# First mixer of a hybrid decoder: two block inversions by joined inverses on VectorE, channel sums by matrix products, sample taps as products and row sums

## The chip, the cores and the metric

The kernel runs on one core of a Trainium2 chip. The metric is device time in microseconds of one launch, the median of several runs. Engines are named as in the profile: PE (TensorE), DVE (VectorE), ACT (ScalarE), POOL (GpSimd) and SP (SyncE, which issues transfers); PEld is PE's weight load.

## The reference

One inference step of a two-layer trunk for two groups that share weights: a prompt of 512 new tokens and 8 samples of 4 new tokens each, 544 tokens in all, 1024 channels, all in float32. Layer 0 mixes with a convolution beside a delta rule, layer 1 with a diagonal state-space system; a feed-forward follows each. What matters here is layer 0's mixer:

```python
p = x @ w_in
pa, pb = p[..., :2 * D_A], p[..., 2 * D_A:]
u = pa[..., :D_A] * sigmoid(pa[..., D_A:])
ext = concatenate([conv_state, u], axis=1)
ya = silu(layer_norm(causal_depthwise(ext, conv_w, conv_b), ln_g, ln_b))  # 31 taps, 512 channels
...
def step(s, inp):                        # delta rule, 8 heads of 64
    sa = einsum('bhvk,bhk->bhv', s, -kk_t)
    s = s * d_t + sa[..., None] * (kk_t * a_t)[:, :, None, :] + v_t[..., None] * k_t[:, :, None, :]
    return s, einsum('bhvk,bhk->bhv', s, r_t)
...
out = concatenate([ya, yb], axis=-1) @ w_out     # ya: convolution, yb: delta rule
```

## The kernel before

Channels stand on partitions, tokens along the rows: 512 prompt columns and 32 sample columns, in two halves of 256 and 288. Every weight product is made of three products of split operands (`xh`, `xl` with `whi`, `wlo`); the weights come as one stream through the whole kernel, and ACT and DVE split each chunk (`split`, L262 and L170).

The first mixer has four pairs of heads and four convolution tiles. For pair p, `pair_in` projects and shifts keys, rates and values, `pair_front` makes products within chunks of 64 tokens (`wkv_front`) and inverts unit lower triangular blocks of 16 (`wkv_solve`), `pair_mid` joins the blocks into inverses of 64 (`wkv_mid`, which reads `mn` from L801 on) and prepares the scan (`wkv_tail`), and `pair_out` runs the scan over 8 chunks, a group norm of the heads and the gate. `sample_front` and `sample_out` do the same for the samples, all heads at once. `conv_in` and `conv_taps` make tile i of the convolution, `conv_end` its layer norm over four tiles, the activation and the first half of the output projection (the k tiles of `ya`). `mixer_ab_out` adds the second half (the k tiles of `yb`).

`wkv_solve` moves blocks so that each stands on one partition: out to memory (`dx`), back into `xb`, 15 steps of a product (`stmp`) and a sum (`mm`) on POOL, a transposed copy (L782), out to memory (`dm`, L783) and back into `mn` (L787). All its transfers are on SP's queue. `xb` and `mm` have one buffer each.

`conv_taps` does 30 multiply-adds (L167) for the prompt columns and 30 for the sample columns, in turns, into `cacc`. `conv_end` sums the four tiles on POOL (into rows of `xres`, which is free until the residual is loaded), one product with a matrix of ones spreads the sum over the channels (L598), and the same again for the squares (L610).

The order of work comes from `weave`: generators are advanced in turns, each step has a priority of its turn plus a delay, and a scheduler orders the instructions of every engine from these priorities; at run time each engine takes its instructions in that fixed order. The delays and the weaves that matter:

```python
hi, md, lo = -4, -6, 8
weave((hi, pair_out(1)), (hi, pair_mid(2)), (md, pair_front(3)), (0, conv_in(3)), (lo, conv_taps(2)))
weave((hi, pair_out(2)), (hi, pair_mid(3)), (md, sample_front()), (lo, conv_taps(3)))
weave((hi, pair_out(3)), (hi, sample_out()), (0, conv_end()))
```

## Time and profile before

| | us |
|---|---|
| median of three runs | 1544.8 |
| lowest and highest run | 1542.68, 1547.15 |
| span of the profiled execution | 1542.7 |

The profile is one execution on the core; its span, from the first to the last instruction, equals the lowest run to the digits shown, so nothing has to be added around it. Times in the rows are microseconds from the span's start. Busy time of an engine doesn't count its register, branch, semaphore and transfer-issuing instructions. In a name such as `cacc<-usam,cols,cacc` the tile written stands left of the arrow. Products with float32 operands leave two records each. `[3.75 <-DMA mn<-dm]` behind a row says that the engine stood idle that long before it, and what ended the wait. The first mixer runs from the start to about 381 us, its layer norm to about 447 us.

### The profile page before, as it was taken

What the parts mean: (1) busy time and instruction counts of PE and PEld (TensorE: products, weight loads), DVE (VectorE), ACT (ScalarE), POOL (GpSimd) and SP (SyncE); (2) the same over time, 40 slices, a digit from 0 to 9 for tenths busy, and PEclk for the clock granted to TensorE, in tenths of its full rate; (3) what the DMA queues carried; (4) which work ended last, traced back from release to release, by engine and by line L of the source; (5) the groups of instructions that cost most, each with busy time, mean ns of one, the idle gap of its engine ahead of it and who ended that gap; (6) DMA issues with size and microseconds to landing.
All of it is one profiled execution on the core that took longest, in us unless ns stands there. A gap on an engine that the chain in (4) does not pass through costs nothing.

```text
span 1542.7 us, 31307 instructions
## 1 busy us (share of the span) xinstructions
PE 1445.0 (94%) x12064; PEld 1374.1 (89%) x12064; DVE 1013.4 (66%) x2513; ACT 616.9 (40%) x1407; POOL 353.9 (23%) x492
## 2 busy tenths in 40 slices
PE   7999999789799999999999789999899999999996
PEld 6988887577789999999899778899899999999996
DVE  6688796766879955557884856754675555554335
ACT  5444352251264444443232435553454444442222
POOL 1252552611540200002561622102420000000102
PEclk9999999689899999999999789999999999999997
DMA  5222113111213232225563367832222222232321
GB/s 192 73 65 67 39 54 100 22 38 58 99 37 118 89 127 89 84 85 164 165 182 116 111 178 210 219 107 96 67 69 89 90 89 85 88 92 86 84 68 58
DMA packets 128340, 152.43 MB, mean 99 GB/s; under 512 B 46512, under 2 KB 71856, under 8 KB 127936
## 3 DMA queue, kind: packets, MB, share of 16 engines
q1 hardware_dynamic: 105232, 120.11, 25.7%
q10 hardware_dynamic: 20800, 22.46, 4.6%
q0 software_dynamic: 2160, 7.87, 1.6%
q8 instruction: 95, 1.56, 0.4%
q14 instruction: 53, 0.43, 0.1%
HBM read 128.17 MB, written 22.22 MB: 97 GB/s over the span
## 4 chain that ended last, share of the span: by engine, by line
PE 71%; DVE 11%; DMA 6%; POOL 4%; issue 3%; ACT 3%; SPq 1%; ACTq 0%; DVEq 0%; POOLq 0%
PE ps_mm L192 61%; PE ps_wk L192 3%; POOL stmp L170 2%; DVE xres L170 2%; POOL mm L170 2%; DVE wlo L170 2%; DVE xres L167 1%; DMA tm<-dk 1%; DVE s5a L170 1%; PE ps_wf L725 1%; ACT xres L164 1%; DVE ln_t L167 1%; PE ps_wk L1089 1%; DMA dg<-s5a 1%; DMA ye<-dy 1%
## 5 line engine op out<-in xcount | busy, mean ns | idle before, releaser
L192 PE MATMUL ps_mm<-xh,whi 128*128 128x256 f32 (+1 forms) x2016 | 492.1, 298 | 21.9 <-ACT whi L262 6.5
L192 PE MATMUL ps_mm<-xl,whi 128*128 128x256 f32 (+1 forms) x2016 | 493.2, 296 | 5.2 <-DVE xl L167 3.6
L192 PE MATMUL ps_mm<-xh,wlo 128*128 128x256 f32 (+1 forms) x2016 | 490.0, 295 | 0.0
L170 DVE TENSOR_TENSOR wlo<-wraw,whi 128x512 fp32r<-128x512 f32 x350 | 258.4, 740 | 272.3 <-ACT whi L262 270.1
L262 ACT CAST whi<-wraw 128x512 fp32r<-128x512 f32 x380 | 230.9, 611 | 514.7 <-PE ps_mm L192 448.9
L192 PEld LDWEIGHTS ps_mm<-xh,whi 128*128 128x128 f32 x2016 | 353.6, 195 | 29.4 <-ACT whi L262 6.8
L192 PEld LDWEIGHTS ps_mm<-xl,whi 128*128 128x128 f32 x2016 | 356.9, 195 | 14.3 <-issue 5.9
L192 PEld LDWEIGHTS ps_mm<-xh,wlo 128*128 128x128 f32 x2016 | 354.3, 194 | 4.6 <-issue 3.9
L192 PE MATMUL ps_mm<-fl,whi 128*128 128x256 f32 (+1 forms) x704 | 154.3, 290 | 0.0
L192 PE MATMUL ps_mm<-fh,whi 128*128 128x256 f32 (+1 forms) x704 | 153.7, 289 | 0.0
L192 PE MATMUL ps_mm<-fh,wlo 128*128 128x256 f32 (+1 forms) x704 | 153.6, 289 | 0.0
L192 PEld LDWEIGHTS ps_mm<-fh,wlo 128*128 128x128 f32 x704 | 115.7, 188 | 0.7 <-issue 0.6
L192 PEld LDWEIGHTS ps_mm<-fl,whi 128*128 128x128 f32 x704 | 115.8, 188 | 0.4 <-issue 0.4
L192 PEld LDWEIGHTS ps_mm<-fh,whi 128*128 128x128 f32 x704 | 115.5, 188 | 0.7 <-issue 0.6
L167 DVE SCALAR_TENSOR_TENSOR c<-ps_mm,cols,c 128x254 f32<-128x254 f32 (+3 forms) x264 | 98.1, 393 | 0.3
L167 DVE SCALAR_TENSOR_TENSOR cacc<-uext,cols,cacc 128x512 f32<-128x512 f32 x120 | 94.8, 790 | 2.5 <-ACT cacc L164 1.5
L170 POOL TENSOR_TENSOR ln_s<-xres 128x256 f32<-128x256 f32 (+1 forms) x8 | 10.3, 1301 | 313.8 <-DVE xres L170 313.8
L170 DVE TENSOR_TENSOR s5a<-s5a 128x64 f32<-128x64 f32 (+3 forms) x135 | 74.5, 574 | 9.0 <-DMA dg<-s5a 4.4
L170 DVE TENSOR_TENSOR c<-ps_mm,c 128x256 f32<-128x256 f32 (+1 forms) x88 | 35.3, 435 | 60.3 <-PE ps_mm L192 54.6
L170 POOL TENSOR_TENSOR s5a<-s5a 128x1024 f32<-128x1024 f32 (+2 forms) x19 | 48.1, 2532 | 49.9 <-DVE s5a L170 44.2
L170 POOL TENSOR_TENSOR wlo<-wraw,whi 128x512 fp32r<-128x512 f32 x30 | 41.5, 1390 | 77.7 <-ACT whi L262 74.2
L192 PE MATMUL ps_mm<-yh,whi 128*128 128x256 f32 (+1 forms) x240 | 57.4, 293 | 0.3 <-ACT sg L164 0.3
(368 smaller groups left out, 2064.2 us busy)
## 6 DMA issues: line engine op xcount, KB each, us to landing
wraw<-in_w_up SPq DMA_DIRECT2D x176, 256.0 KB
wraw<-in_w_down SPq DMA_DIRECT2D x80, 256.0 KB
wraw<-in_w_in_ab SPq DMA_DIRECT2D x44, 256.0 KB
wraw<-in_w_out_c SPq DMA_DIRECT2D x21, 256.0 KB
wraw<-in_w_out_ab SPq DMA_DIRECT2D x16, 256.0 KB
dg<-s5a ACTq DMA_DIRECT2D x8, 512.0 KB
df<-s5a ACTq DMA_DIRECT2D x8, 512.0 KB
gx<-dg POOLq DMA_DIRECT2D x8, 512.0 KB, 5.1
```

What stands on the lines that cost most here:

```text
L164: return self.nc.scalar.activation(out, in_, f, **k)
L167: return self.nc.vector.scalar_tensor_tensor(out, a, s, b, op0, op1)
L170: return (eng or self.nc.vector).tensor_tensor(out, a, b, op=op)
L192: ins = self.nc.tensor.matmul(*a, **k)
L262: self.nc.scalar.copy(hi, src)
L725: nc.tensor.matmul(pa[:, i], lhsT=flat(kb[HS[hd], c // 2, c % 2]), rhs=ar[HS[hd], :, c], start=True, stop=True)
L1089: gate = nc.tensor.matmul(pq[:, 4 * i + j:4 * i + j + 1], lhsT=t[:, b - P:b], rhs=self.con("ones")[:, 0:1], start=t is ts[0], stop=t is ts ...
```

## The change

Three parts of the first mixer are written anew; the rest of the kernel stays as it was.

1. The inversions of pair 3 and of the samples (`late`) go by joining: the inverse of a block of 2s comes from its two diagonal inverses of size s, for s = 2, 4, 8, with the 2-blocks written directly. Each level is a product per block, a row sum, a product per block, a row sum, all on DVE; the transposed copy is on ACT. The loads and returns of these two alternate between SP's and ACT's queues. Their products use a tile `spr` of one buffer.
2. The sample taps of a convolution tile become two POOL products over all 31 taps (two tokens of every sample at a time, into `spr`), two DVE row sums and a bias on ACT.
3. `conv_end` sums four tiles, and then their squares, by four products that accumulate in one bank; the POOL sums are gone, and it uses rows 3 to 7 of `xres` instead of 5 to 7.

`sample_front` moves from the weave of `pair_mid(3)` into that of `pair_front(3)`, at the same delay.

```diff
             self.act(ca, uext[:, 0:NP], AF.Identity, scale=w(0), bias=cb)
-            self.act(cs, usam[:, 0:32], AF.Identity, scale=w(0), bias=cb)
+            at = usam[:, 0:8]
+            o = COL["caw"] + i * 31
+            ws = self.cols[:, o:o + 31].unsqueeze(1).unsqueeze(1).broadcast_to([P, 2, NS, 31])
+            for j in range(0, NJ, 2):
+                pr = gp.tile([P, 512], F32, name="spr", tag="spr", bufs=1)
+                pr = pr[:, 0:2 * NS * 31].rearrange("p (j s t) -> p j s t", s=NS, t=31)
+                win = bass.AP(at.tensor, at.offset + NS * j, [at.ap[0], (NS, 2), (1, NS), (NS, 31)])
+                self.tt(pr, win, ws, ALU.mult, nc.gpsimd)
+                nc.vector.tensor_reduce(cs[:, NS * j:NS * j + 2 * NS].rearrange("p (j s) -> p j s", s=NS), pr,
+                                        mybir.AxisListType.X, ALU.add)
+            self.act(cs, cs, AF.Identity, bias=cb)
             for t in range(1, 31):
...
                 self.stt(ca, uext[:, t:t + NP], w(t), ca, ALU.mult, ALU.add)
-                self.stt(cs, usam[:, 8 * t:8 * t + 32], w(t), cs, ALU.mult, ALU.add)
             yield
...
             yield from self.wkv_front(d, dx)
-            yield from self.wkv_solve(dx, dm, 8, self.mn)
+            yield from self.wkv_solve(dx, dm, 8, self.mn, p == 3)
...
             yield from self.sample_in(g, dx)
-            yield from self.wkv_solve(dx, dm, 4, self.mns)
+            yield from self.wkv_solve(dx, dm, 4, self.mns, True)
...
         def conv_end():
-            s1, q, t = row(5), row(6), row(7)
+            s1, sqs = row(3), [row(4 + i) for i in range(4)]
             for h in range(2):
                 n, H = HB[h], HT[h]
-                self.tt(s1[:, H], cacc[:, 0, H], cacc[:, 1, H], ALU.add, nc.gpsimd)
-                for i in (2, 3):
-                    self.tt(s1[:, H], s1[:, H], cacc[:, i, H], ALU.add, nc.gpsimd)
                 pm = self.bank([P, 512], "wf")
-                nc.tensor.matmul(pm[:, :n], lhsT=self.con("ones"), rhs=s1[:, H], start=True, stop=True)
+                for i in range(4):
+                    nc.tensor.matmul(pm[:, :n], lhsT=self.con("ones"), rhs=cacc[:, i, H], start=i == 0, stop=i == 3)
                 for i in range(4):
                     self.stt(cacc[:, i, H], pm[:, :n], -1.0 / 512, cacc[:, i, H], ALU.mult, ALU.add)
-                    if i == 0:
-                        self.act(q[:, H], cacc[:, i, H], AF.Square)
-                    else:
-                        self.act(t[:, H], cacc[:, i, H], AF.Square)
-                        self.tt(q[:, H], q[:, H], t[:, H], ALU.add, nc.gpsimd)
+                    self.act(sqs[i][:, H], cacc[:, i, H], AF.Square)
                 yield
...
                 pv = self.bank([P, 512], "wf")
-                nc.tensor.matmul(pv[:, :n], lhsT=self.con("ones"), rhs=q[:, H], start=True, stop=True)
+                for i in range(4):
+                    nc.tensor.matmul(pv[:, :n], lhsT=self.con("ones"), rhs=sqs[i][:, H], start=i == 0, stop=i == 3)
                 root = self.act(s1[:, H], pv[:, :n], AF.Sqrt, scale=1.0 / 512, bias=self.eps(LN_EPS))
...
         weave((hi, pair_out(0)), (hi, pair_mid(1)), (md, pair_front(2)), (0, conv_in(2)), (0, after(4, pair_in(3))), (lo, conv_taps(1)))
-        weave((hi, pair_out(1)), (hi, pair_mid(2)), (md, pair_front(3)), (0, conv_in(3)), (lo, conv_taps(2)))
+        weave((hi, pair_out(1)), (hi, pair_mid(2)), (md, pair_front(3)), (md, sample_front()), (0, conv_in(3)), (lo, conv_taps(2)))
         nc.scalar.dma_start(out=O["shift"], in_=shout)
-        weave((hi, pair_out(2)), (hi, pair_mid(3)), (md, sample_front()), (lo, conv_taps(3)))
+        weave((hi, pair_out(2)), (hi, pair_mid(3)), (lo, conv_taps(3)))
         weave((hi, pair_out(3)), (hi, sample_out()), (0, conv_end()))
...
-    def wkv_solve(self, dx, dm, nu, mn):
+    def wkv_solve(self, dx, dm, nu, mn, late=False):
         nc, gp = self.nc, self.gp
...
         tmp = gp.tile([64, 64], F32, name="stmp", tag="stmp", bufs=2)
+        queue = lambda q: nc.scalar if late and q % 2 else nc.sync
         src = dx.rearrange("(q r) u c -> q u r c", r=16)
...
             b = q % nb
-            nc.sync.dma_start(out=xb[q * nu:(q + 1) * nu], in_=src[q][:, :, 16 * b:16 * b + 16])
+            queue(q).dma_start(out=xb[q * nu:(q + 1) * nu], in_=src[q][:, :, 16 * b:16 * b + 16])
         M = mm[:n, 0]
...
         nc.gpsimd.memset(mm[:n, 0].rearrange("p a b -> p (a b)")[:, 0:256:17], 1.0)
-        for j in range(15):
+        if late:
+            V = nc.vector
+            ap = lambda t, o, *d: bass.AP(t.tensor, t.offset + o, [t.ap[0], *d])
+            X = xb[:n]
+            V.tensor_copy(ap(M, 16, (34, 8)), ap(X, 1, (34, 8)))
+            for s in (2, 4, 8):
+                k, d = 8 // s, 34 * s
+                pr = gp.tile([P, 512], F32, name="spr", tag="spr", bufs=1)[:n, :k * s ** 3]
+                T = tmp[:n, :k * s * s]
+                for g in range(k):
+                    o, r = d * g, slice(g * s ** 3, (g + 1) * s ** 3)
+                    self.tt(pr[:, r].rearrange("p (i b j) -> p i b j", b=s, j=s),
+                            ap(X, o + s, (1, s), (0, s), (16, s)), ap(M, o, (0, s), (1, s), (16, s)), ALU.mult)
+                V.tensor_reduce(T, pr.rearrange("p (i j) -> p i j", j=s), mybir.AxisListType.X, ALU.add)
+                for g in range(k):
+                    o, r = d * g, slice(g * s ** 3, (g + 1) * s ** 3)
+                    self.tt(pr[:, r].rearrange("p (i b j) -> p i b j", b=s, j=s),
+                            ap(M, o + 17 * s, (16, s), (0, s), (1, s)), ap(T, g * s * s, (0, s), (1, s), (s, s)), ALU.mult)
+                V.tensor_reduce(ap(M, 16 * s, (d, k), (16, s), (1, s)),
+                                pr.rearrange("p (g i b j) -> p g i b j", g=k, i=s, j=s), mybir.AxisListType.X, ALU.add)
+            yield
+        for j in range(0 if late else 15):
             rows, cols = 15 - j, j + 1
...
                 yield
-        nc.gpsimd.tensor_copy(mm[:n, 1].rearrange("p a b -> p b a"), M)
+        if late:
+            nc.scalar.copy(mm[:n, 1].rearrange("p a b -> p b a"), M)
+        else:
+            nc.gpsimd.tensor_copy(mm[:n, 1].rearrange("p a b -> p b a"), M)
         nc.sync.dma_start(out=dm.rearrange("q u w r c -> (q u) (w r c)"), in_=mm[:n].rearrange("p w a b -> p (w a b)"))
...
             o = 64 * (q // nb) + 16 * b
-            nc.sync.dma_start(out=mn[o:o + 16, :, :, 16 * b:16 * b + 16].rearrange("r u w c -> r (u w) c"),
+            queue(q).dma_start(out=mn[o:o + 16, :, :, 16 * b:16 * b + 16].rearrange("r u w c -> r (u w) c"),
                               in_=dm[q].rearrange("u w r c -> r (u w) c"))
...
...
```

## Rows read from the trace of the kernel before

**Rows 1.** The page: the span, then busy time of each engine

```profile
span 1542.7 us, 31307 instructions
...
PE 1445.0 (94%) x12064; PEld 1374.1 (89%) x12064; DVE 1013.4 (66%) x2513; ACT 616.9 (40%) x1407; POOL 353.9 (23%) x492
```

**Rows 2.** By stretch: PE, PEld, DVE, ACT, POOL busy (instructions), clock, DMA, GB/s

```profile
251.00:297.00 46.00, 38.37 (x447) 28.17 (x446) 40.84 (x93) 12.71 (x29) 21.82 (x40) 0.83 0.22 60
297.00:320.00 23.00, 16.44 (x225) 11.81 (x225) 14.48 (x26) 10.72 (x23) 15.06 (x39) 0.72 0.15 32
320.00:381.00 61.00, 59.02 (x687) 48.81 (x686) 39.26 (x115) 14.97 (x40) 6.04 (x7) 0.95 0.14 46
```

**Rows 3.** Timeline of POOL, 200 to 385 us: start, duration, line, operation, [idle before it]

```profile
265.99 1.06 POOL L170 TENSOR_TENSOR xres<-xres,cacc 128x256 f32<-128x256 f32 x1
...
275.79 0.21 POOL L170 TENSOR_TENSOR stmp<-xb,mm 64x15 f32<-64x15 f32 x1 [2.69 <-DMA xb<-dx]
...
292.69 0.61 POOL L782 COPY mm<-mm 64x256 f32<-64x256 f32 x1
...
301.17 0.20 POOL L170 TENSOR_TENSOR stmp<-xb,mm 16x15 f32<-16x15 f32 x1 [2.76 <-DMA xb<-dxs]
...
316.79 0.60 POOL L782 COPY mm<-mm 16x256 f32<-16x256 f32 x1
```

**Rows 4.** Timeline of the SP queue, 200 to 330 us

```profile
270.89 2.88 SPq L770 DMA_DIRECT2D xb<-dx  x8
...
295.64 3.74 SPq L787 DMA_DIRECT2D mn<-dm  x8
```

**Rows 5.** Timeline of PE, 290 to 336 us

```profile
298.84 0.66 PE L801 MATMUL ps_wo<-mn,xa 64*64 64x64 f32 x4 [3.75 <-DMA mn<-dm]
...
302.48 1.60 PE L801 MATMUL ps_wo<-mn,xa 64*64 64x64 f32 x24
...
309.69 0.67 PE L610 MATMUL ps_wf<-xres,cons 128*128 128x256 f32 x2 [0.26 <-DVE cacc L167]
...
314.00 0.75 PE L610 MATMUL ps_wf<-xres,cons 128*128 128x288 f32 x2 [2.10 <-POOL xres L170]
...
319.63 0.58 PE L192 MATMUL ps_mm<-xh,whi 128*128 128x256 f32 x1 [1.97 <-ACT xh L262]
```

**Rows 6.** Timeline of DVE, 225 to 325 us

```profile
242.69 0.69 DVE L170 TENSOR_TENSOR z<-ps_wo,cons 128x512 f32<-128x512 f32 x1 [4.34 <-PE ps_wo L801]
...
265.36 3.03 DVE L167 SCALAR_TENSOR_TENSOR cacc<-uext,cols,cacc 128x512 f32<-128x512 f32 x3
...
296.11 0.75 DVE L167 SCALAR_TENSOR_TENSOR cacc<-uext,cols,cacc 128x512 f32<-128x512 f32 x1
...
312.78 1.75 DVE L612 RECIPROCAL xres<-xres 128x256 f32<-128x256 f32 x1 [1.21 <-ACT xres L164]
```

**Rows 7.** Timeline of DVE, 324 to 400 us

```profile
374.31 0.15 DVE L170 TENSOR_TENSOR rq_t<-rq_y 128x2 f32<-128x2 f32 x1
374.50 0.16 DVE L167 SCALAR_TENSOR_TENSOR rq_t<-rq_t,rq_x 128x2 f32<-128x2 f32 x1
```

**Rows 8.** Instructions that write cacc: duration in ns min/median/max, first and last start

```profile
L167 DVE SCALAR_TENSOR_TENSOR cacc<-usam,cols,cacc x120: 226/243/1348, 16.3 to 262.2; 128x32 f32<-128x32 f32 x120
```

**Rows 9.** POOL groups by shape, 0 to 390 us: busy, mean ns, idle before

```profile
L170 POOL TENSOR_TENSOR sm<-swv,cons 128x512 f32<-128x512 f32 x2 | 2.1, 1042 | 31.3 <-DVE swv L170 31.3
```

**Rows 10.** The chain that ended last: start, duration, what

```profile
19.02 1.46 DVE cacc L167 x9
```

**Rows 11.** The same chain, 200 to 450 us

```profile
320.21 3.74 PE ps_wo L840 x32
...
328.81 1.08 PE ps_wo L865 x32
...
330.77 1.02 PE ps_wo L859 x16
...
380.93 7.93 PE ps_mm L192 x40
```

## The prediction

> **What bounds the kernel now.** I read the page first: PE is busy for 94% of the span [rows 1], so a change pays only where PE stands still, runs at a lower clock, or has work taken away. Then the table by stretch for the end of the first mixer, where both late inversions stand. From 251 to 320 us PE is idle for 7.6 + 6.6 us and the granted clock is 0.83 and 0.72; from 320 to 381 us it is idle for 2.0 us at 0.95 [rows 2]. What could come back at most: 16.2 us of idle time, plus 38.4 x 0.17 + 16.4 x 0.28 + 59.0 x 0.05 = 14 us if all products there ran at the full one of the two levels (2.4 instead of 1.2 GHz). That is 30 us; no part of this change can be worth more in this stage.
>
> Then the timelines of this stretch, to see which waits end last. Two chains run side by side. The first is pair 3's inversion: its blocks lie in `xb` at 275.8, POOL needs until 293.3 for 31 small instructions (17.5 us) [rows 3], the result goes out and comes back in eight transfers that take SP 3.74 us to issue [rows 4], and PE, waiting 3.75 us, starts on it at 298.8 and gets the rest at 302.5 [rows 5]. The sample's inversion stands behind it, 301.2 to 317.4 on the same engine [rows 3]. The second is the convolution: the last prompt tap ends on DVE at 296.9 [rows 6], the layer norm over four tiles follows, with POOL sums between the sample's inversion steps (PE waits 2.1 us for one), and the first product of the output projection starts at 319.6, after 2 us of waiting for its operand [rows 5]. From there PE has 61 us of nearly gapless work up to 380.9, where the second half of the output projection begins [rows 11]. So the stage ends sooner if the point 319.6 comes sooner, or if work that now lies behind it is done in the idle time ahead of it.
>
> **The late inversions move to DVE.** Out: 31 POOL instructions for pair 3 and 31 for the sample. In, for each: one copy, then three levels of products and row sums, (4+1+4+1) + (2+1+2+1) + (1+1+1+1) = 20, together 21 DVE instructions, and the transpose as one ACT copy. Seventeen have at most 128 elements a row; dependent ones of that kind start 0.19 us apart [rows 7]: 3.2 us. Four read or write 512; a 128x512 product took 0.69 us [rows 6]: 2.8 us. So 6.0 us instead of 17.5 and 16.2. No `tensor_reduce` stands in the trace. Its bounds: as cheap as a small instruction (0.19), or as dear as the dearest one-input DVE row, the reciprocal, 1.75 us for 256 elements, 3.5 for 512 [rows 6]; an inversion then costs between 5 and 12 us. I take the product's price, because both stream 512 values through one instruction.
>
> The order changes too. The sample's front is woven beside pair 3's, and its solve is emitted first. `xb`, `mm` and `spr` have one buffer each, so pair 3's load waits until the sample's blocks were read, and its memset until the sample's inverse went out. I reckon pair 3's start as 3.5 us later for that (half of a solve, between nothing and one whole solve plus the 2.3 us from copy to first return transfer [rows 3, 4]). The two queues share the eight loads and the eight returns, which saves half of 2.88 and of 3.74 us of issue [rows 4], 3.3 us. With 17.5 - 6.0 = 11.5 us less in the solve and 3 us lost to taps that stand between its steps (four of 0.75 [rows 6]), the inverse reaches PE 11.5 + 3.3 - 3.5 - 3 = 8 us earlier, near 294. What queues behind: ACT's queue now holds waits for transfers (eight issues per solve), and the weight casts behind them; ACT is busy 12.7 of 46 us there [rows 2], so I price that at nothing, and at up to 2 us if casts stall PE.
>
> **Sample taps.** Out: 120 DVE instructions of 0.24 us [rows 8] and four ACT starts. In: eight POOL products of 496 elements, eight DVE sums, four ACT biases. Most of the 120 run far ahead of their turn (from 16.3 us on) in DVE's idle time and cost little; after 251 us only four are left. One place is on the chain: nine of them, 1.46 us at 19.0 [rows 10]; the new product reads the last window column, so it can't run there. Gain 1.5 us (between 0 and 2). A POOL product of this size took 1.04 us [rows 9]; the far bounds are the solve's smallest step, 0.20, and twice the price for its strided pattern. What hides them is POOL's free time: it is busy 21.8 of the 46 us before 297 even with pair 3's solve on it [rows 2]. Without that cover the solves of pairs 1 and 2, which stay on POOL, lose 2 us each.
>
> The Trainium skill (SBUF, State Buffer, section on the single rule of contention) says that a two-input VectorE operation and a GpSimd operation that reads SBUF lock each other out for a whole instruction. Here three taps took 3.03 us instead of 2.25 while two POOL sums ran [rows 3, 6], 0.4 us for each. By the rule the two POOL products of tile 3 would hold up its taps by 2.1 us, by the row by 0.8, and the gain would be 1.3 us smaller by the rule; I keep the row.
>
> **What DVE carries.** It was busy 40.8 of 46 us up to 297 [rows 2]. Added before the last tap: two solves 12.0, two sums 1.4, POOL's interference 0.8; gone: four sample taps, 1.0. Of the 5.2 idle us I let 4.2 fill. The last tap then ends at 296.9 + 9 = 306.
>
> **Layer norm.** Out: six POOL sums ahead of the first product pair and six ahead of the second. In: twelve more products with float32 operands; one costs PE 0.75 us at the clock of then [rows 5], 9 us in all, at most 18 at the lower level and about half when they follow each other. Three of four in the first group need only tiles 0 to 2 and run in idle PE time; that idle time is the cover, and without it the 9 us stand on PE. After the last tap: one product 0.75, four subtractions and squares that follow one another (two of a tap's length, 1.5), the last square's product 0.67, together 3 us, then as now from the end of the first half's product, 310.4, to 319.6: 9.3 us [rows 5]. So the projection starts at 306 + 12.3 = 318.3 instead of 319.6: 1.3 us gained. The row places 3 to 7 are held longer, and five loads of the residual wait on SP until the norm is through; tile 3 needs its row only three projection tiles later, so I price that at nothing, at 2 us if not.
>
> **Work pulled ahead.** With the inverse 8 us earlier and the sample's some 20 us earlier, PE does in front of 318 what stood behind it: the 32 products of 3.74 us, two times 16 and 32 products of about 1.0 and 1.1 us [rows 11], 7.9 us, and the sample's first products, which I put at 2 us (estimate: two groups of 16 like the sixteen of 1.02). Together 9.9 us of the 61. Bounds: 0, if that time is used up by waits, and 20, if the whole scan comes forward.
>
> **Sum.** 1.5 (start) + 1.3 (projection) + 9.9 (pulled ahead) = 12.7 us. The profiled span of 1542.7 equals the fastest of the three runs (1542.68), so nothing is added around it; the median of the runs, 1544.8, lies 2.1 above. 1542.7 - 12.7 + 2.1 = 1532.1.
>
> **Rivals.** (A) Both chains come forward fully: the solves slip between taps that had idle time anyway, the last tap ends at 300 and the clock stays up. The 12.7 us grow by 6 and by half of the 14 us of clock: 1519. For it: PE's low clock is in just this stretch. Against it: DVE has 5.2 idle us for 13 us of work. (B) Nothing measurable: pair 3 waits for the whole solve of the sample through the shared tiles. If the sample's blocks come as late as today's place behind pair 3's, the inverse of pair 3 lands near 301 again, the products pulled ahead shrink to the sample's 2 us, and 1.5 + 1.3 + 2 is left less 3 for ACT's waits: 1543. (C) Slower: DVE becomes the bound. If a solve costs 12 us (the dear row sums), the last tap ends at 318 instead of 306, the projection starts at 330, 10.7 us later than now, and 5 us are pulled ahead: 10.7 - 5 - 1.5 = 4 us slower, and 3 us more if POOL products delay the middle solves: 1549 to 1552. It decides from a last tap at about 312 on.
>
> **Chances.** Forecast 0.45, own range 1524 to 1538; A 0.12; B 0.23; C 0.20. A difference under 0.3% (4.6 us) can't be told from none: the three runs lie that far apart. Of B, 0.03 falls on the faster and 0.02 on the slower side. Faster 0.60, same 0.18, slower 0.22. The range goes from just under A, 1517, to C's upper end, 1552, which leaves out about 0.15.
>
> **What the new profile would show.** Right: DVE does `spr` products and sums for two solves in about 6 us each, POOL's `stmp` groups fall from 75 to 45, the inverse reaches PE (the products on `mn`) before 296, the last tap of tile 3 ends at 303 to 308, the first output projection product starts by 319, and the second half of the projection before 371 instead of 380.9. The step most likely to be wrong is the last tap's time: every DVE microsecond added ahead of it delays the projection. The forecast fails if that tap ends after 312, if a row sum of 496 elements costs well over 1 us, or if the pulled-ahead products still stand behind the projection's start in PE's order.

## The result, and the profile after

The changed kernel takes 1553.65 us (median of nine runs, 1547.29 to 1573.25), the kernel before 1545.81 us beside it (nine runs, 1541.54 to 1548.85). The ratio is 1.0057, with a 95% interval of 1.0034 to 1.0081: slower, where 1532.1 was forecast, and 1.65 us outside the range. In the ratios here and below, runs over 1.5% above the fastest of the same kernel are left out.

The page of the changed kernel and the three stretches answer to [rows 1, 2]:

```profile
span 1550.5 us, 31231 instructions
...
PE 1453.7 (94%) x12088; PEld 1381.7 (89%) x12088; DVE 1005.7 (65%) x2443; ACT 619.6 (40%) x1409; POOL 330.4 (21%) x426
```

```profile
251.00:297.00 46.00, 38.16 (x378) 27.02 (x377) 37.80 (x105) 11.82 (x27) 2.01 (x4) 0.75 0.12 28
297.00:320.00 23.00, 16.60 (x202) 11.96 (x202) 20.15 (x37) 9.69 (x20) 3.00 (x2) 0.83 0.25 62
320.00:381.00 61.00, 60.67 (x688) 51.55 (x689) 30.68 (x86) 16.37 (x43) 4.82 (x5) 0.89 0.12 37
```

From 251 to 320 us POOL has 5.0 us of work instead of 36.9. But PE does 580 products there instead of 672, and what it did not do stands behind.

Of the two solves, these are DVE's first instruction of the sample's, one that stands in it and waits for PE, its last, the first of pair 3's, and then the whole of pair 3's last level, with all that DVE does between its steps:

```profile
263.14 0.56 DVE L785 COPY mm<-xb 16x8 f32<-16x8 f32 x1 [2.41 <-DMA xb<-dxs]
...
272.36 0.42 DVE L170 TENSOR_TENSOR xp<-ps_wo,pend 128x256 f32<-128x256 f32 x1 [2.83 <-PE ps_wo L896]
...
281.86 0.67 DVE L799 TENSOR_REDUCE mm<-spr 16x64 f32<-16x512 f32 x1
...
285.56 0.15 DVE L785 COPY mm<-xb 64x8 f32<-64x8 f32 x1
...
295.26 1.00 DVE L170 TENSOR_TENSOR spr<-xb,mm 64x512 f32<-64x512 f32 x1
296.18 0.15 DVE L167 SCALAR_TENSOR_TENSOR rq_y<-rq_t,rq_y 128x8 f32<-128x8 f32 x1
296.26 0.27 DVE L167 SCALAR_TENSOR_TENSOR st<-ps_wb,pend,xp 128x64 f32<-128x64 f32 x1
296.45 0.73 DVE L167 SCALAR_TENSOR_TENSOR cacc<-uext,cols,cacc 128x512 f32<-128x512 f32 x1
297.11 0.67 DVE L794 TENSOR_REDUCE stmp<-spr 64x64 f32<-64x512 f32 x1
297.71 0.15 DVE L170 TENSOR_TENSOR rq_t<-rq_y 128x8 f32<-128x8 f32 x1
297.78 0.74 DVE L167 SCALAR_TENSOR_TENSOR cacc<-uext,cols,cacc 128x512 f32<-128x512 f32 x1
298.44 1.06 DVE L170 TENSOR_TENSOR spr<-mm,stmp 64x512 f32<-64x512 f32 x1
299.43 0.15 DVE L167 SCALAR_TENSOR_TENSOR rq_t<-rq_t,rq_x 128x8 f32<-128x8 f32 x1
299.50 0.74 DVE L167 SCALAR_TENSOR_TENSOR cacc<-uext,cols,cacc 128x512 f32<-128x512 f32 x1
300.17 0.67 DVE L799 TENSOR_REDUCE mm<-spr 64x64 f32<-64x512 f32 x1
```

Between two steps of the solve stands a tap of 0.73 us. Pair 3's solve is about 6.0 us of work, but it lasts 15.3 us, from 285.56 to 300.84, because twelve taps and sixteen small instructions of the scan and the head norm stand in it. Neighbouring records overlap by some 0.07 us, so the parts are counted from start to start: the steps take 5.2 us, the taps 7.9, the small instructions 2.0, and DVE idles for 0.1. POOL took 17.5 [rows 3].

And it starts 9.8 us later than POOL did (285.56 against 275.79), because the sample's solve holds `xb` and `mm` from 263.14 on. That one lasts 19.4 us: steps 5.6, twelve taps 8.0, other instructions 2.9, and 2.8 us in which DVE, in its fixed order, waits for PE with `xp`. The 9.8 us are a net figure: the new taps bring the work ahead of this point forward. With taps and sums alone (`no_solves`, below) pair 3's solve starts at 268.38, so the two inversions, moved to DVE and turned round, cost this start 17.2 us.

The transfers on the queues of SP and ACT, one bias on ACT, and POOL:

```profile
277.72 1.37 SPq L776 DMA_DIRECT2D xb<-dx  x4
...
303.91 1.78 SPq L818 DMA_DIRECT2D mn<-dm  x4
```

```profile
303.87 1.88 ACTq L818 DMA_DIRECT2D mn<-dm  x4
306.29 0.32 ACT L164 ACTIVATE cacc<-cacc,cols 128x32 f32<-128x32 f32 x1 [3.20 <-DMA mn<-dm]
```

```profile
284.90 0.31 POOL L778 MEMSET mm<- 64x256 f32 x1 [11.76 <-DMA dms<-mm]
...
300.92 1.50 POOL L170 TENSOR_TENSOR spr<-usam,cols 128x496 f32<-128x496 f32 x1 [15.53 <-DVE rq_y L167]
303.63 1.50 POOL L170 TENSOR_TENSOR spr<-usam,cols 128x496 f32<-128x496 f32 x1 [1.21 <-DVE cacc L443]
```

The memset of pair 3's `mm` waits 11.76 us for the sample's inverse to leave it. The sample products of tile 3 wait 15.53 us for `spr` until pair 3's solve is done with it; the wait is put down to a `rq_y` of DVE that ends in the same tenth of a microsecond as the solve. The bias is put down to the return transfer, but the row sum that it reads ends only at 306.26. PE, answering to [rows 5] (L832 is L801 of before, L606 and L615 are L598 and L610, L871 and L896 are L840 and L865):

```profile
300.30 1.22 PE L606 MATMUL ps_wf<-cacc,cons 128*128 128x256 f32 x2 [5.09 <-DVE cacc L167]
...
306.58 0.41 PE L832 MATMUL ps_wo<-mn,xa 64*64 64x64 f32 x4
306.93 0.75 PE L606 MATMUL ps_wf<-cacc,cons 128*128 128x288 f32 x2
...
309.50 1.99 PE L615 MATMUL ps_wf<-xres,cons 128*128 128x256 f32 x8
...
314.15 2.10 PE L615 MATMUL ps_wf<-xres,cons 128*128 128x288 f32 x8
...
320.25 1.08 PE L862 MATMUL ps_wo<-n,x 32*32 32x32 f32 x32 [3.35 <-ACT x L858]
321.26 0.39 PE L192 MATMUL ps_mm<-xh,whi 128*128 128x256 f32 x1
...
326.25 3.12 PE L871 MATMUL ps_wo<-R,n 64*64 64x128 f32 x30
...
333.24 0.69 PE L896 MATMUL ps_wo<-wv,xk 128*64 128x64 f32 x16
...
389.49 0.39 PE L192 MATMUL ps_mm<-xh,whi 128*128 128x256 f32 x1 [0.83 <-DVE yb L170]
```

The inverse reaches PE 7.7 us later than before, the projection starts 1.6 us later, and its second half 8.6 us later (389.5 against 380.9). The products of pair 3 that stood behind the projection's start before (L840 to L865 in [rows 11]) still stand there, 4 to 6 us later, at a granted clock of 0.89 instead of 0.95. The first half of the projection is through at 381.8, and the second half then stands behind what this chain and the sample's leave in `yb` (last row). The span is 7.8 us longer.

### The profile page after: what moved, and what is told of

Read it like the earlier page. It is cut to its first block, busy times and chain, and to the rows that moved or that the text cites. A ratio compares the mean times of both kernels' runs of the same rounds, so it can differ in the third digit from the quotient of the medians.

```text
span 1550.5 us, 31231 instructions
## 1 busy us (share of the span) xinstructions
PE 1453.7 (94%) x12088; PEld 1381.7 (89%) x12088; DVE 1005.7 (65%) x2443; ACT 619.6 (40%) x1409; POOL 330.4 (21%) x426
## 4 chain that ended last, share of the span: by engine, by line
PE 75%; DVE 11%; DMA 4%; issue 2%; ACT 2%; POOL 2%; SPq 0%; ACTq 0%; DVEq 0%; POOLq 0%
PE ps_mm L192 62%; PE ps_wk L192 3%; DVE xres L170 2%; DVE xres L167 2%; DVE wlo L170 1%; PE ps_wf L730 1%; DVE s5a L170 1%; POOL stmp L170 1%; DVE ln_t L167 1%; POOL mm L170 1%; PE ps_wk L1120 1%; DMA ye<-dy 1%; PE ps_wi L699 1%; DMA tm<-dk 1%; DMA dy<-yg 1%
## 5 line engine op out<-in xcount | busy, mean ns | idle before, releaser
L170 DVE TENSOR_TENSOR wlo<-wraw,whi 128x512 fp32r<-128x512 f32 x350 | 253.6, 726 | 279.0 <-ACT whi L262 276.3
```

Of the source, the lines that this page charges most:

```text
L170: return (eng or self.nc.vector).tensor_tensor(out, a, b, op=op)
```

## The experiments

Theory S, from these profiles: the late inversions, by their place on DVE and by their new order, carry the loss; taps and sums gain or are neutral. Rivals: the POOL products of the taps or the float32 products of the sums cost it; or holds of shared tiles and queues alone do, and an inversion on DVE pays in itself.

The table holds all kernels. The four times are those of the points that [rows 5, 6, 11] show for before, each read from PE's and DVE's timelines of the one profile: the first product on pair 3's `mn`, the end of tile 3's last tap, the first product of the projection, and the first of its second half. Ratios are to the kernel before on the same chip, five rounds each but for the whole change.

| kernel | `mn` | last tap | projection | 2nd half | ratio | 95% |
|---|---|---|---|---|---|---|
| before | 298.8 | 296.9 | 319.6 | 380.9 | | |
| before_again | 299.3 | 297.3 | 320.1 | 381.2 | 0.9998 | 0.9975, 1.0021 |
| whole change | 306.6 | 300.2 | 321.3 | 389.5 | 1.0057 | 1.0034, 1.0081 |
| taps_only | 292.3 | 296.4 | 320.7 | 379.4 | 1.0011 | 0.9993, 1.0029 |
| sums_only | 297.6 | 293.1 | 320.1 | 379.6 | 1.0010 | 0.9994, 1.0025 |
| move_only | 312.6 | 299.2 | 321.6 | 387.8 | 1.0041 | 1.0026, 1.0056 |
| solves_moved | 316.1 | 302.2 | 323.3 | 392.2 | 1.0070 | 1.0051, 1.0088 |
| no_solves | 291.4 | 291.6 | 312.3 | 374.6 | 0.9957 | 0.9937, 0.9977 |
| solves_second | 301.5 | 305.3 | 331.5 | 387.3 | 1.0001 | 0.9974, 1.0027 |
| own_tiles | 300.0 | 298.2 | 322.7 | 379.6 | 1.0022 | 0.9991, 1.0052 |
| quiet | 308.7 | 325.7 | 350.8 | 395.6 | 1.0006 | 0.9976, 1.0035 |
| tap_tile | 310.5 | 304.2 | 324.8 | 387.1 | 1.0027 | 1.0003, 1.0052 |
| sp_only | 306.2 | 299.2 | 323.2 | 384.0 | 1.0038 | 1.0017, 1.0059 |
| own_all | 315.9 | 312.5 | 330.7 | 393.9 | 1.0041 | 1.0015, 1.0068 |
| pair3_dve | 302.4 | 305.8 | 327.6 | 385.6 | 1.0003 | 0.9977, 1.0030 |
| sample_dve | 290.5 | 294.9 | 319.5 | 380.7 | 1.0017 | 0.9995, 1.0040 |
| solves_in_place | 305.4 | 304.3 | 328.0 | 393.6 | 1.0091 | 1.0060, 1.0122 |

**The kernel before, once more** (no edit).

> The kernel before, unchanged. Nothing is left out. It shows how far two sets of runs of one kernel lie apart, and how far one profile lies from another. Expected: ratio 1.000 with an interval of 0.002 to either side; last tap, first projection product, second half of the projection and the first product of the feed-forward within 1.5 us of the first profile (296.9, 319.6, 380.9, 427.1). If those points of one and the same kernel lie 4 us or more apart, the profiles of the partial kernels can't carry differences of that size, and only the timed ratios can.

The four points lie within 0.5 us of the first profile; the first product of the feed-forward lies 4.5 us off (422.6 against 427.1). So the profiles can't be compared behind the projection's second half.

Ahead of it, one repetition is not the whole noise. POOL writes the transposed copy of pair 2's inverse at 224.5 us in the whole change and at 225.2 to 225.9 in the seven other kernels with the new taps that agree on it, but at 228.2 in own_all, 228.6 in tap_tile and 230.0 in quiet, although DVE, ACT and POOL take the same instructions in the same order as in the whole change up to 242 us. From 100 to 200 us the granted clock is 0.98 in the whole change, 0.95 in own_all and tap_tile and 0.93 in quiet. So 3.7, 4.1 and 5.5 us of these three kernels' points in the table do not come from their edits; lengths within a profile are safer than points.

**One part alone.** taps_only: before with the new `conv_taps`. sums_only: before with the new `conv_end`.

> The kernel before with the sample taps as products and row sums, and nothing else. Theory S (the late solves lose the time): the taps give the 1.5 to 2.5 us that the changed kernel is ahead at 110 us and lose nothing later, so 0 to 3 us faster than before. Rival N (the norm chain loses it, because tile 3's sample sums come late): 2 to 5 us slower than before, since the taps' sums still stand ahead of the norm.

> The kernel before with the four-product sums in the convolution's end, and nothing else. Theory S: within 2 us of before, the POOL sums' wait of 2.1 us goes and the extra products take its place. Rival N (twelve more float32 products on PE and the order around them lose the time): 4 to 8 us slower.

Neither can be told from no change by its time; in the profiles both bring the second half forward, by 1.5 and 1.3 us. The rival that blames the sums (4 to 8 us) falls. The one that blames the taps (2 to 5 us) does not fall by this time, 1.7 us slower with an interval of 2.8 to either side; it falls with no_solves, below.

move_only: before, with both inversions still on POOL, and this:

```diff
-        weave((hi, pair_out(1)), (hi, pair_mid(2)), (md, pair_front(3)), (0, conv_in(3)), (lo, conv_taps(2)))
+        weave((hi, pair_out(1)), (hi, pair_mid(2)), (md, pair_front(3)), (md, sample_front()), (0, conv_in(3)), (lo, conv_taps(2)))
...
-        weave((hi, pair_out(2)), (hi, pair_mid(3)), (md, sample_front()), (lo, conv_taps(3)))
+        weave((hi, pair_out(2)), (hi, pair_mid(3)), (lo, conv_taps(3)))
```

> The kernel before with the sample front woven beside pair 3's front, both solves still on POOL. Theory S says the shared tiles serialise the two solves with the sample's first: pair 3's inverse reaches PE about 10 us later or more (a solve of 16 us goes ahead of it), so 5 to 12 us slower. Rival M0: the order of the two is harmless, within 2 us.

The order alone costs 0.41%, as theory S had it (5 to 12 us). POOL now does the sample's solve first, and pair 3's tile is cleared only when the sample's inverse has left it:

```profile
289.86 0.31 POOL L773 MEMSET mm<- 64x256 f32 x1 [5.25 <-DMA dms<-mm]
...
290.58 0.21 POOL L170 TENSOR_TENSOR stmp<-xb,mm 64x15 f32<-64x15 f32 x1 [0.23 <-POOL mm L774]
```

In before this step ran at 275.79 [rows 3]: 14.8 us of delay, and the inverse is 13.7 us later at PE.

solves_moved: the whole change without taps and sums.

> The changed kernel without its taps and without its sums: the late solves on VectorE and the moved sample front only. Theory S: this part carries the loss, 6 to 12 us slower than before. Rival N: within 3 us of before.

0.70% slower: with the order, the inversions on DVE add 0.29% to move_only; the two intervals just overlap.

**Order and place apart.** no_solves: taps and sums alone, the inversions on POOL in the old order. solves_second: the whole change with `sample_front` back in its old weave. Besides that weave, no_solves has this against the whole change:

```diff
-            yield from self.wkv_solve(dx, dm, 8, self.mn, p == 3)
+            yield from self.wkv_solve(dx, dm, 8, self.mn)
-            yield from self.wkv_solve(dx, dm, 4, self.mns, True)
+            yield from self.wkv_solve(dx, dm, 4, self.mns)
```

> The changed kernel with both solves back on POOL and the sample front in its old place: taps and sums only. Theory S (solves and their move carry the loss): the feed-forward begins 3 to 6 us earlier than before, and the whole is 0 to 6 us faster than before. Rival I (taps and sums hurt once they stand together, through POOL and the norm): 2 to 6 us slower than before.

> The changed kernel with the sample front back in its old weave, so pair 3's solve on VectorE comes first and the sample's second. Theory O (the order through the shared tiles is the loss): pair 3's inverse reaches PE before 300 us instead of 306.6, and the whole is 6 to 12 us faster than the changed kernel, so at or below before. Rival D (VectorE's added work is the loss): within 4 us of the changed kernel.

no_solves is 0.43% faster than before, and so beats both kernels (1541.38 us against 1547.60 beside it). Taps and sums each gave nothing alone, so the parts do not add; why they gain only together no run shows. Its stretches, POOL's solve of pair 3 from first step to transposed copy, and PE:

```profile
251.00:297.00 46.00, 39.95 (x446) 28.32 (x444) 39.74 (x82) 12.77 (x30) 26.83 (x57) 0.85 0.18 37
297.00:320.00 23.00, 21.70 (x283) 17.25 (x282) 16.55 (x37) 16.98 (x41) 3.77 (x13) 0.85 0.22 66
```

```profile
268.38 0.21 POOL L170 TENSOR_TENSOR stmp<-xb,mm 64x15 f32<-64x15 f32 x1 [4.43 <-DMA xb<-dx]
...
284.56 1.12 POOL L813 COPY mm<-mm 64x256 f32<-64x256 f32 x1
```

```profile
291.39 0.41 PE L832 MATMUL ps_wo<-mn,xa 64*64 64x64 f32 x4 [2.38 <-DMA mn<-dm]
...
312.27 0.38 PE L192 MATMUL ps_mm<-xh,whi 128*128 128x256 f32 x1 [1.05 <-ACT xh L262]
```

POOL's solve starts 7.4 us earlier than before, the last tap ends 5.3 us and the projection starts 7.4 us earlier, and PE does 726 products from 251 to 320 us instead of 672 (the two rows count three at their border twice). Put the two inversions on DVE in that same order (solves_second), and the last tap ends 13.7 us and the projection starts 19.2 us later; the ratio rises from 0.9957 to 1.0001. That is the price of DVE in the old order. The new order adds another 0.56%: the whole change has 1.0057. So theory O, that the order is the loss, is half of it: the time that it forecast for the old order came (6 to 12 us less than the whole change), though the inverse came at 301.5 and not before 300.

**One inversion at a time**, in no_solves' order. pair3_dve has `p == 3` back, sample_dve has `True` back; solves_in_place is before with both on DVE.

> The whole change in the old order, with pair 3's inversion alone on DVE and the sample's on POOL. Nothing is left out. Theory D (the inversion's 21 dependent steps stand in DVE's fixed order with a tap of 0.73 us between them, so it lasts 15 to 21 us although it is busy for 6, no less than POOL's 17.3): the inverse of pair 3 reaches PE at 292 to 301 against 291.4 with POOL, the last tap ends 5 to 8 us later than 291.6, the second half of the projection starts 2 to 8 us later than 374.6, ratio to the kernel before 0.997 to 1.001. Rival P (an inversion on DVE pays as predicted, only the sharing of DVE by two of them costs): the inverse at PE before 288, ratio 0.990 to 0.995.

> The whole change in the old order, with the sample's inversion alone on DVE and pair 3's on POOL. Nothing is left out. Theory D: pair 3's inverse at PE within 2 us of 291.4; the sample's small steps stand among the last taps or the layer norm's steps, the last tap ends 0 to 6 us later than 291.6 and the first projection product 2 to 8 us later than 312.3; ratio 0.996 to 1.000. Rival P: the sample's inverse comes some 8 us earlier and PE does its products ahead of the projection; the second half of the projection before 373, ratio 0.991 to 0.995.

> The kernel before with both late inversions on DVE in the old order; the sample taps, the sums and the order stay as before. Nothing is left out. Theory D: last tap at 305 to 311 (before 296.9), first projection product at 326 to 333 (before 319.6), second half of the projection 4 to 9 us after 380.9, ratio 1.002 to 1.006. Rival P: the inverse at PE before 293, projection at or before 319, ratio 0.993 to 0.998.

Theory D holds in sign in all three and was too mild in most of its figures: pair 3's solve alone moves the second half by 11.1 us, the sample's by 6.1, both without the other edits by 12.6, with 0.9% in the time. By time alone, sample_dve (1.0017) and pair3_dve (1.0003) are each slower than no_solves (0.9957), all three measured against before. Rival P falls: pair 3's inverse from DVE is at PE 11.0 us later (pair3_dve against no_solves) and 6.6 us later (solves_in_place against before), and the sample's solve ends at 304.4 in sample_dve, at 301.2 on POOL in no_solves. In pair3_dve the solve lasts from 273.14 to 294.59, 21.5 us, where POOL took 17.3:

```profile
273.14 0.17 DVE L785 COPY mm<-xb 64x8 f32<-64x8 f32 x1 [0.65 <-DMA xb<-dx]
...
293.92 0.67 DVE L799 TENSOR_REDUCE mm<-spr 64x64 f32<-64x512 f32 x1
```

Counted from start to start, the 21.5 us are 5.3 of steps, 7.9 of twelve taps, 5.2 of other instructions and 3.0 in which DVE waits for PE. Of the 11.0 us by which the inverse is later at PE, the longer solve is 4.2; its start is 4.8 later and the way from its end to PE 2.1 longer. The start is not the taps' doing: the blocks go out 3.3 us later, and the loads on ACT's queue are issued up to 271.9, where SP's queue is through at 269.1.

So one inversion on DVE costs even alone, which is the part of the loss that the order does not carry. From no_solves to the whole change the ratio rises by 1.0%: order and inversions lose that, and taps and sums give 0.4% back.

**Holds.** own_tiles, tap_tile and sp_only each take one hold out of the whole change; own_all takes out all three.

```diff
-            yield from self.wkv_solve(dx, dm, 4, self.mns, True)
+            yield from self.wkv_solve(dx, dm, 4, self.mns, True, (row(7), row(6)))   # own_tiles: xb, mm
-                pr = gp.tile([P, 512], F32, name="spr", tag="spr", bufs=1)
+                pr = row(5) if i == 3 else gp.tile([P, 512], F32, name="spr", tag="spr", bufs=1)   # tap_tile
-        queue = lambda q: nc.scalar if late and q % 2 else nc.sync
+        queue = lambda q: nc.sync   # sp_only
```

In own_tiles `wkv_solve` takes the two rows and uses them in place of its own tiles.

> The changed kernel with block and inverse tiles of the sample's solve in two free rows of the residual's place, so pair 3's load and memset need not wait for it; the product tile stays shared. Theory O: pair 3's solve starts near 276 instead of 285.6, its inverse reaches PE near 297, and 4 to 8 us come back. Rival A (VectorE's alternation of solve steps and taps sets the pace): the two solves now share VectorE with the taps, the inverse comes at most 3 us earlier and 0 to 2 us come back.

> The whole change, but the products of tile 3's sample taps get a row of their own instead of the one product tile that pair 3's inversion also writes. Nothing is left out. In the changed kernel these two products wait for that tile until 300.9 us and their sums end at 306.3, while the layer norm's sample half waits for them. Theory Q (the shared tile and the return transfers in ACT's queue hold the same point one behind the other, so that taking one away moves it only to the other): the products run before 292, the sums before 296, but the bias, behind the four returns in ACT's queue, still runs at about 305.8, and the first product of the projection moves by at most 1 us (320.3 to 321.5); the ratio to the kernel before stays at 1.004 to 1.007. Rival Q1 (the shared tile alone holds the norm): projection 3 to 5 us earlier, at 316 to 318, ratio 1.001 to 1.004.

> The whole change, but all block loads and returns of the two late inversions are issued on SP's queue, none on ACT's. Nothing is left out. Theory Q: ACT no longer holds the last square, the bias and the weight casts behind returns, but the bias still waits for the sums that end at 306.3, and pair 3's blocks and inverse come 1.4 and 1.9 us later (half of the loads and of the returns that ACT issued): the inverse at PE at about 310, the first product of the projection within 1 us of 321.3, the ratio 1.004 to 1.008. Rival Q2 (waits in ACT's queue, which the prediction priced at nothing, are the loss): projection at 316 to 318 and the ratio at or under 1.003.

> The whole change with both of the last two edits and with the sample's block and inverse tiles in rows of their own: no tile is shared between the two inversions but the small product tile, and no transfer of theirs stands in ACT's queue. Nothing is left out. Theory Q: with both holds gone the sample half of the norm comes forward, and with its own tiles pair 3's inverse is at PE near 301; the projection's first product at 317 to 319.5, and the ratio 0.999 to 1.002, so still above the kernel with both inversions on GpSimd (0.9957), because the 12 us of inversion on DVE among the taps stay. Rival P (sharing and queues are the whole loss, the inversions on DVE themselves pay as predicted): the ratio falls to 0.992 to 0.996.

With tiles of its own the sample's solve no longer holds pair 3's: the inverse is 6.5 us earlier at PE than in the whole change, the second half 9.9 us earlier, 1.3 ahead of before. The ratio, 1.0022, is not told apart from the whole change's. tap_tile and sp_only do not bring the projection forward, as theory Q had it; they put it 3.5 and 1.9 us later, but 4.1 and 0.9 of that stood there at pair 2's copy. Theory Q's reason fails in tap_tile: the bias, which was to wait for the return transfers until 305.8, ran at 272.11, and the projection is no earlier for it. In sp_only the second half is 5.5 us earlier. Both ratios overlap the whole change's. So neither hold is shown to be the loss by itself. own_all went against theory Q: last tap 312.5, projection 330.7, not 317 to 319.5, of which 3.7 stood there at pair 2's copy. The scheduler had written another order for DVE, in which the sample's solve ran from 266.51 to 294.06 and pair 3's, which shares the small product tile with it, behind it. A hold taken away changes the order as well, so these four runs carry less than the ones before.

**Taps held back.** quiet: the whole change, with tile 3's taps from the fourth on behind the last row sum of the sample's inversion (`solved[4]`), and from the tenth on behind pair 3's (`solved[8]`).

```diff
-                self.stt(ca, uext[:, t:t + NP], w(t), ca, ALU.mult, ALU.add)
+                tap = self.stt(ca, uext[:, t:t + NP], w(t), ca, ALU.mult, ALU.add)
+                if i == 3 and t in (4, 10):
+                    self.chain([self.solved[4 if t == 4 else 8], tap])
```

> The changed kernel with tile 3's taps 4 and later held behind the sample's solve, and taps 10 and later behind pair 3's. Theory A (taps between the solve's steps): each solve takes under 10 us instead of 19 and 15, and pair 3's inverse reaches PE 6 to 10 us earlier; taps end later, and the whole comes 0 to 6 us faster than the changed kernel. Rival C (the convolution's chain sets the end): the last tap comes 6 us or more later and the whole is 3 to 8 us slower than the changed kernel.

Part of the sample's solve, then what it waits for, then the first and last step of pair 3's:

```profile
276.59 0.39 DVE L170 TENSOR_TENSOR spr<-mm,stmp 16x8 f32<-16x8 f32 x4
277.01 0.17 DVE L802 TENSOR_REDUCE mm<-spr 16x16 f32<-16x32 f32 x1
277.22 0.43 DVE L170 TENSOR_TENSOR spr<-xb,mm 16x64 f32<-16x64 f32 x2
...
285.98 0.43 DVE L170 TENSOR_TENSOR xp<-ps_wo,pend 128x256 f32<-128x256 f32 x1 [5.50 <-PE ps_wo L899]
...
292.82 0.16 DVE L788 COPY mm<-xb 64x8 f32<-64x8 f32 x1
...
301.48 0.68 DVE L802 TENSOR_REDUCE mm<-spr 64x64 f32<-64x512 f32 x1
```

Where no tap stands between them, dependent steps follow each other within 0.04 us. Pair 3's solve now has three taps in it instead of twelve and lasts 9.3 us instead of 15.3: nine taps of 0.66 us from start to start are the 6.0 us of difference. This is the direct test of the taps between the steps, and theory A's "under 10 us" holds for this solve. It fails for the sample's, which lasts 16.5 us with no tap in it, 6.7 of them waits of DVE for PE (5.50 in the row above).

The taps are then late: the last one ends at 325.7, and the projection starts at 350.8, 25 and 30 us later than in the whole change, where 5.5 stood there at pair 2's copy. The profiled execution took 1563.1 us, the longest of its twelve runs. By their times quiet has 1.0006, lower than the whole change's 1.0057, with intervals that just touch; so against the whole change holding the taps back costs nothing in time and may gain. Why so late a projection costs the time so little is open, as is the same gap, smaller, for solves_second.

## Why the prediction was wrong

**The start, 1.5 us: right where it was read.** ACT's activation into `k` near 34 us starts at 33.36 instead of 34.87, 1.5 us earlier. The lead grows: pair 2's solve starts at 206.48 instead of 214.24, tile 3's first tap at 257.65 instead of 260.92. That none of it is lost by the end no run shows; taps_only has the lead as well (206.81) and is no faster.

**The solve's work, 6.0 us: right.** Its row sums of 512 values took 0.67 us, not the 3.5 of the dear bound, and its products of 512 took 1.00 to 1.07 instead of 0.69.

**"The inverse reaches PE 11.5 + 3.3 - 3.5 - 3 = 8 us earlier, near 294": the step that failed.** The 294 is counted from 302.5, where PE did the rest of the products before; from the first product, 298.8, the same sum gives 290.5. The first product came at 306.6 and the rest at 307.6, so 7.7 and 5.1 us later instead of 8.3 earlier. Three terms were mis-sized. "3 us lost to taps that stand between its steps", four of 0.75: twelve taps and sixteen small instructions, 9.9 us. "3.5 us later" for the shared tiles: 9.8 us, since the sample's solve ahead of it was stretched in the same way, and by a wait for PE. 3.3 us saved by the two queues: from the end of the solve to PE it took 5.7 us against 5.5; without the transposed copy, which ACT now makes behind the solve in 0.63 us, 5.0, so half a microsecond. In sum, 9.8 later, 15.3 - 17.5 = 2.2 shorter, 0.2 longer on the way: the 7.7, but for rounding. Rival B had the shared tiles' part of this mechanism, with 301.

**Work pulled ahead, 9.9 us: none.** It hung on that step: the rows of L871 and L896 above are the products that were to come forward. From the projection's first product to the second half, 61.3 us of before were to become 51.4; they became 68.2, with PE's 699 products there against 686 before.

**The projection at 318.3: 321.3, only 3 us off by luck.** Two errors cancel in part. The last tap came at 300.2 instead of 306: the two row sums ran behind it (1.3 us), the 30 taps from 251 us on took 736 ns on average instead of 819 (2.5 us in all), and the first of them started 3.3 us earlier; that is 1.3 us more than the difference, and what took it back was not traced. But the norm took 21.0 us from there, not 12.3. Before, the same interval is 296.9 to 319.6, 22.8 us, and both its ends stand in [rows 5, 6]; the prediction rebuilt it from a part of it (3 us to the end of the first half's product, which took 13.5 before). It fell by 1.7 us; with the new sums alone (sums_only) it is 27.0. Over all kernels of the table it lies between 18 and 27 us.

**Rival C came nearest in time, 1.65 us short, and not by its mechanism.** A row sum of 496 took 0.66 us, and the last tap ended well before 312. What is true of it is that DVE is where the time goes.

**ACT's waits at nothing:** open. In sp_only, without transfers on ACT's queue, the projection is no earlier, but the second half is, by 5.5 us in the one profile; the times can't tell it from the whole change. In pair3_dve loads on ACT's queue were issued up to 2.8 us behind those on SP's.

**Sample taps.** DVE's row sum 0.66 us as priced (0.69), the POOL product dearer than 1.04:

```profile
L170 POOL TENSOR_TENSOR spr<-usam,cols x8: 1457/1586/2024, 62.1 to 303.6; 128x496 f32<-128x496 f32 x8
L443 DVE TENSOR_REDUCE cacc<-spr x8: 656/658/670, 64.9 to 305.6; 128x16 f32<-128x496 f32 x8
```

What stays open: why the loss of solves_second and quiet is smaller in their times than in their profiles, why taps and sums gain only together, how the loss splits between longer solves, held tiles and queues, and what sets the granted clock in this stage (0.75, 0.83 and 0.89 after, 0.83, 0.72 and 0.95 before).

## What to carry to other kernels

A chain of short dependent steps costs on an engine with a fixed order what stands between its steps, too: price it as steps plus one neighbour per step, from the rows of the engine that it moves to, and add what such a neighbour waits for. Moving it from an engine with free time to the one that carries the other late chain costs both. When an order is turned round, look first for the tiles with one buffer: the whole stretched chain of the one ahead is the delay of the other. Read an interval whose two ends stand in the trace from the trace, before building it from parts. Before two kernels' points are compared, compare a point that neither edit touches.

## What the runs showed of the hardware

The 30 taps of 512 took 736 ns on average in the whole change, where POOL is busy for 2.0 us from 251 to 297, 804 in no_solves, where it is for 26.8, and 819 before:

```profile
L167 DVE SCALAR_TENSOR_TENSOR cacc<-uext,cols,cacc 128x512 f32<-128x512 f32 x30 | 22.1, 736 | 0.6 <-ACT cacc L164 0.6
```

```profile
L167 DVE SCALAR_TENSOR_TENSOR cacc<-uext,cols,cacc 128x512 f32<-128x512 f32 x30 | 24.1, 804 | 0.4
```

The 2.0 us between them look like the price of POOL's solve, but it is two taps that carry most of it. In no_solves the 17 taps beside steps of the solve alone take 755 ns on average, and before, the 15 such taps take 744, against 750 and 745 with nothing beside them. The long taps stand beside long POOL instructions:

```profile
257.81 1.51 POOL L170 TENSOR_TENSOR spr<-usam,cols 128x496 f32<-128x496 f32 x1 [0.78 <-DVE cacc L443]
262.54 1.42 POOL L170 TENSOR_TENSOR yb<-yb,v 128x544 f32<-128x544 f32 x1 [3.22 <-ACT yb L527]
```

```profile
258.50 1.37 DVE L167 SCALAR_TENSOR_TENSOR cacc<-uext,cols,cacc 128x512 f32<-128x512 f32 x1
```

The first of these taps ends at 259.87, 0.55 us behind the end of the POOL product that ran when it started; another, from 262.80 to 264.51, ends 0.55 us behind the second. Before, the five long taps of tile 3 (1.08 to 1.49 us, beside POOL's sums and the same `yb` product) each end 0.55 us behind the POOL instruction that ran when they started. The tap from 262.03 to 262.77, which had started ahead of the `yb` product, took its usual 0.74 us. So the longer a POOL instruction still has to run when a tap could start, the more the tap pays: with 0.82 and 1.16 us left the two taps took 0.62 and 0.96 us longer than the usual 0.75, where the prediction charged 0.4. The whole change did not pay this for the sample products of tile 3, which ran behind the last tap. In POOL's solve POOL's own steps of one shape last 0.28 us at one time and 0.62 to 0.76 at another, so there the wait falls on POOL. The Trainium skill (SBUF — State Buffer, section Who interferes with whom) says that issue order decides which of the two blocks; the trace agrees, as these taps show. So its rule, which the prediction set aside for the 0.4 us of a row, is the nearer of the two.

A row sum of 512 float32 values took 0.67 us, the product of 512 with both inputs in SBUF and repeated strides 1.00 to 1.07, and the product of 512 of [rows 6] 0.69. The Trainium skill (VectorE: DVE Perf Modes, section Rules for kernel authors) calls the row sum the slowest operation of the engine; in this kernel's shapes it is not, and the measurement decides.
